# Whole-page gathers, input rows in three token tiles whose space the split output weights take, and first attention units without pacing

## The chip, the cores and the metric

The kernel runs on one core of a Trainium2 chip. The metric is device time in microseconds, from the first to the last instruction of one launch with what lies around it. The engines are TensorE (PE; its weight loads are shown as PEld), VectorE (DVE), ScalarE (ACT), GpSimd (POOL) and SyncE (SP). Each runs its own list of instructions in order. DMAs are issued from SP, ACT or POOL and run on 16 DMA engines. SyncE computes nothing; most DMAs are issued from it.

## What is computed

One step of a hybrid decoder layer, for a prompt of 1024 tokens and for 8 sample sequences of one new token each, all in float32. The reference, cut to what matters here:

```python
hn = rms_norm(x, norm_g)                           # 1024 + 8 rows of 1024
u, v, z_a, q, kc, vc, ks, vs, kw, vw, g, z_b = split(hn @ w_in)
a_out = u * spatial_gate(layer_norm(v)) * silu(z_a)
# per head: three attentions, weighted by gates and added
#   compressed blocks of kc/vc, selected blocks of ks/vs, a window of 512 of kw/vw
mix = concat([a_out, o_b * silu(z_b)], -1)
y = rms_norm(x + mix @ w_out, final_g)
# sample rows: k and v of the past come from pages, cache[page_table], 2 pages of 128 tokens each
pages = lambda c: c[page_table].reshape(B, past, N_KV, HEAD_DIM)
```

Two key/value heads serve 8 query heads. `compress` multiplies overlapping blocks of 32 keys with a weight. With 16 blocks of 64 tokens and 16 selected, every causal block is selected. Outputs are y for both parts and the new cache rows.

## The kernel before

**Products.** A float32 product is made from halves: each operand is split into a rounded float32r part ("hi") and the rest ("lo"), and three products hi·hi, hi·lo, lo·hi are added in PSUM. ACT makes hi by a cast, DVE or POOL makes lo by a subtraction.

**Stages** (times of the profiled execution). 0 to 116 us: `xw` (input rows transposed, next to the first weights) is loaded for eight slices k of the model dimension; the rows, times the norm weight, become `xh` and `xl` (lines 211, 212), each a tile of 8 x 1032 columns (1024 prompt tokens and 8 sample tokens). Feature tiles (`pf`) multiply 128 weight columns with all tokens in three pieces of `CH` = 344 columns. Then come token-major projections, nine row tiles each (eight of the prompt, one of the samples): V of the gMLP (`ptv`, with gate products `pg`), K tiles (`pta`, followed by transposes `pkt`), V tiles (`ptb`). From about 255 us `compress` runs for keys and values (transposes `pct`, product `pc`), then `sample_attention` (`pA`, `pB`, `pT`, `po`). From 361 us the prompt's attention runs in 32 units of two heads: eight blocks qb of 128 queries, four units each. A unit has scores (`S`), exponentials on ACT, weights times gate on DVE or POOL, transposes (`pt`) and values (`o`). The scores of unit i+1 are made while the values of unit i run. A score row covers 128 (qb+1) selected keys, up to 5 x 128 window keys and 64 compressed ones.

**Fill.** The remaining feature tiles (`feature_tiles`, two more u, three z and four b) are traced as fill for compress, the samples and the first 16 units. Later the output projection (`output`, `project`, `pout`) is the fill of units 18 to 31. Fill is traced with the lowest priority; a scheduler, when the program is built, sets the fixed order of each engine. `paced()` keeps fill products of a unit behind the last value product of the unit before (line 1196), and `held_back` (line 1200) keeps output products behind the last value product of unit 17.

**Pages and output weights.** `early(t, behind)` (line 386) is called once per row tile of V, K and V again, t = 0 to 23, behind a cast on ACT. It issues from ACT: the store of the last finished lo half of an output weight piece (line 389), page gathers (`gather`, lines 381 and 383), and for t < 16 the load of a 128 x 512 piece of `w_out` (line 398), which ACT casts (401) and POOL subtracts (402). The gather of a compressed page writes 256 rows of 512 bytes to `cg`; the gather of a selected page takes the two halves of 128 rows (k and p) and writes 512-byte rows to `kg`, so that `compress` and `sample_attention` read 8 KB rows (lines 688, 770, 795). When all 16 early units are traced, `woh` and `wol` take the space of `xh` and `xl` (tags wh and wl): `w_out` is loaded a second time, cast again on ACT (line 1205), and the lo halves are read back (1207).

Of the kernel before, what the change touches and what calls it, by code (L numbers as in the profile page):

```python
# [17 lines left out]
KT = 8  # L18
CH = 344
# [20 lines left out]
def trunk(tc, io, outs):  # L40
# [7 lines left out]
    with ExitStack() as top:  # L48
# [26 lines left out]
        cg = dram.tile([2, P, 16, P], F32, name="cg")  # L75
        kg = dram.tile([2, P, 16, P], F32, name="kg")
        wol_d = dram.tile([2, P, KT, 512], F32, name="wol_d")
# [53 lines left out]
        RSv = [RS[:, j * CH:(j + 1) * CH] for j in range(3)]  # L131
# [18 lines left out]
        def f_tiles(n):  # L150

            return [(ps_b if n % 2 else ps_s)("pf")[:, 0:CH] for _ in range(3)]
# [6 lines left out]
        def f_mm(hi, lo, outs, k, thirds=(0, 1, 2)):  # L159
            for (w, x, n) in ((hi, xh, 0), (hi, xl, 1), (lo, xh, 2)):  # L160
                for out, j in zip(outs, thirds):
                    last = mm(out, w, x[:, k, j * CH:(j + 1) * CH],
                       start=(k == 0 and n == 0), stop=(k == KT - 1 and n == 2))
            return last

        def views(t2d):
            return [t2d[:, j * CH:(j + 1) * CH] for j in range(3)]
# [30 lines left out]
        for k in range(KT):  # L198
# [5 lines left out]
            cuts = (0, wx + CH, wx + 2 * CH, wx + TT) if k == 0 else (0, wx + TT)  # L204
# [19 lines left out]
        first = [f_tiles(0), f_tiles(1), [ps_o("pf")[:, 0:CH], ps_p("pf")[:, 0:CH]]]  # L224
# [33 lines left out]
        rest = ps_s("pf")[:, 0:CH]  # L258
# [11 lines left out]
        g.tensor_copy(xsS[:, :, 0:8], f32(xh[:, :, T:TT]))  # L270
        xs_copy = g.tensor_copy(xsS[:, :, 32:40], f32(xl[:, :, T:TT]))
# [21 lines left out]
        for a, b in ((0, 2 * CH), (2 * CH, TT)):  # L293
            v.scalar_tensor_tensor(uz[:, 1, a:b], uz[:, 1, a:b] if a == 0 else rest, 0.5, RS[:, a:b],
                                   op0=ALU.mult, op1=ALU.mult)
# [83 lines left out]
        def gather(n):  # L379
            if n < 16:  # L380
                s.dma_start(cg[:, :, n, :], io["cA"][bass.ds(prow[n], 1)].rearrange("o k p c -> (o k) p c"))
            else:
                s.dma_start(kg[:, :, n - 16, :],
                            io["cB"][bass.ds(prow[n - 16], 1)].rearrange("o p (k c) -> (o k) p c", k=2))

        def early(t, behind):
            with tc.issue_after(behind.ins):
                if wo_low:
                    s.dma_start(*wo_low.pop())
                if t < 8:  # L390
# [4 lines left out]
                if t < 16:  # L395
                    half, k = t % 2, t // 2
                    st = wo.tile([P, 512], F32, tag="wost", name="wost")
                    s.dma_start(st, io["w_out"][k, :, half * 512:half * 512 + 512])
                    hi = wo.tile([P, 512], F32R, tag="wohi", bufs=1, name="wohi")
                    lo = wo.tile([P, 512], F32R, tag="wolo", name="wolo")  # L400
                    s.copy(hi, st)
                    g.tensor_tensor(lo, st, f32(hi), op=ALU.subtract)
                    wo_low.append((wol_d[half, :, k, :], f32(lo)))
# [7 lines left out]
        def t_tile(ps, wts, i, cols):  # L411
            if i < 8:
                sl = slice(i * P, (i + 1) * P)
                for k in range(KT):
                    hi, lo = wts[k]
                    mm(ps[:, :cols], xh[:, k, sl], hi[:, :cols], k == 0, False)
                    mm(ps[:, :cols], xh[:, k, sl], lo[:, :cols], False, False)
                    mm(ps[:, :cols], xl[:, k, sl], hi[:, :cols], False, k == KT - 1)
# [188 lines left out]
        def feature_tiles(bank):  # L607
# [5 lines left out]
            for n, (what, i, _) in enumerate(todo):  # L613
                wts = f_ahead.pop(0)
                if 0 < n < len(todo) - 1:
# [3 lines left out]
                for j in range(3):  # L619
                    ps = bank()("pf")[:, 0:CH]  # L620
                    for k in range(KT):
                        hi, lo = wts[k // 4]
                        c = (k % 4) * P
                        with tc.high_priority(FILL), paced():
                            at_bank[1] = f_mm(hi[:, c:c + P], lo[:, c:c + P], [ps], k, (j,))
                        if k % 2:
                            yield
                    if what == "u":
                        v.scalar_tensor_tensor(views(u)[j], ps, 0.5, RSv[j], op0=ALU.mult, op1=ALU.mult)
                        continue  # L630
                    n_p = CH if j < 2 else T - 2 * CH
                    cols = slice(j * CH, j * CH + n_p)
                    if what == "z":
                        gt = ftp.tile([P, CH], F32, tag="gt", bufs=2, name="gt")
                        sy.dma_start(gt[:, 0:n_p], sd[i, :, cols])
# [703 lines left out]
```

## Time and profile before

| | us |
|---|---|
| three runs | 743.98, 746.26, 746.06; median 746.06 |
| the profiled execution | 744.38 |
| its span, first to last instruction | 742.6 |
| PE busy | 693.6 |
| DVE busy | 509.1 |
| ACT busy | 383.0 |
| POOL busy | 293.1 |
| granted TensorE clock, mean | 0.967 |

The span holds 12,587 instructions and 91.29 MB of DMA traffic. PE's ends are modelled, so a busy PE may still be waiting a little. A granted clock of 1.00 is the upper level, 2.4 GHz; 0.50 is 1.2 GHz; a value between is a mean over the stretch.

### The profile page before, as it was taken

Reading aid. Unit: us, or ns where it says so; the run is one execution under the profiler, and the core shown is the slowest. Engines: PE = TensorE matmul, PEld = TensorE weight load, DVE = VectorE, ACT = ScalarE, POOL = GpSimd, SP = SyncE. Lnnn points to the kernel's source line nnn. Section 1 sums busy time; section 2 is a strip of 40 time slices with the busy share of each in tenths; the row PEclk is TensorE's granted clock in tenths of the full one; section 3 lists DMA queues with packets and bytes.
Section 4 is the critical chain, followed back from the end, with each engine's and each line's share of the span. In section 5 each row is a group of like instructions: output and inputs, shape, how many; then the busy total and the mean of one; then the engine's idle time right before and its main releaser. Section 6 shows DMA issues by size and latency. Waiting matters only on the chain.

```text
span 742.6 us, 12587 instructions
## 1 busy us (share of the span) xinstructions
PE 693.6 (93%) x4186; PEld 636.6 (86%) x4186; DVE 509.1 (69%) x1470; ACT 383.0 (52%) x906; POOL 293.1 (39%) x282
## 2 busy tenths in 40 slices
PE   9999998999779769999899999988999999999994
PEld 7999986889669769879799999967888988899893
DVE  5848883698362257542699878887868787878743
ACT  7614312232353454311577867797656675767631
POOL 0034224456122213333222544444756565556511
PEclk9999998999999979999799999998999999999997
DMA  9334655333654464172532112299133021122011
GB/s 330 105 141 171 164 125 159 118 107 122 215 162 147 133 190 161 48 294 72 145 90 78 62 49 63 78 387 263 44 101 99 31 85 60 44 72 72 15 57 56
DMA packets 69096, 91.29 MB, mean 123 GB/s; under 512 B 5872, under 2 KB 45408, under 8 KB 68232
## 3 DMA queue, kind: packets, MB, share of 16 engines
q1 hardware_dynamic: 55496, 75.48, 32.3%
q10 hardware_dynamic: 13376, 12.85, 5.5%
q0 software_dynamic: 160, 2.15, 0.8%
q8 instruction: 33, 0.54, 0.3%
q14 instruction: 31, 0.25, 0.1%
HBM read 67.85 MB, written 28.91 MB: 130 GB/s over the span
## 4 chain that ended last, share of the span: by engine, by line
PE 67%; DVE 9%; DMA 9%; issue 6%; ACT 4%; ACTq 2%; POOL 1%; SPq 0%; POOLq 0%; DVEq 0%
PE pf L45 15%; PE pout L45 12%; PE o L45 10%; PE S L45 9%; PE pt L978 8%; PE ptv L45 3%; PE pta L45 3%; DMA wst<-in_wF 2%; PE pg L45 2%; PE pc L45 2%; DVE wlo L144 2%; DMA wost<-in_w_out 1%; DMA wst<-in_w_c 1%; PE po L45 1%; DMA kg<-in_cB 1%
## 5 line engine op out<-in xcount | busy, mean ns | idle before, releaser
L982 DVE TENSOR_TENSOR tl<-pt,th 128x512 fp32r<-128x512 f32 (+1 forms) x160 | 101.1, 644 | 19.1 <-ACT th L981 18.2
L45 PE MATMUL pf<-xh,whi 128*128 128x344 f32 x384 | 109.0, 328 | 1.5 <-DVE mS L848 0.8
L45 PE MATMUL pf<-xl,whi 128*128 128x344 f32 x384 | 110.2, 325 | 0.0
L45 PE MATMUL pf<-xh,wlo 128*128 128x344 f32 x384 | 109.3, 324 | 0.0
L981 ACT CAST th<-pt 128x512 fp32r<-128x512 f32 (+1 forms) x160 | 85.0, 552 | 36.4 <-PE pt L978 30.7
L955 POOL TENSOR_TENSOR Pw<-Pw,r 128x640 f32<-128x640 f32 (+3 forms) x112 | 76.4, 701 | 49.6 <-DVE r L949 21.9
L45 PE MATMUL pout<-woh,mix 128*128 128x512 f32 (+1 forms) x272 | 88.3, 391 | 2.2 <-ACT mix L1015 1.8
L955 POOL TENSOR_TENSOR Pl<-Pl,r 128x384 f32<-128x384 f32 (+5 forms) x36 | 49.1, 1364 | 87.3 <-DVE r L949 56.0
L45 PE MATMUL o<-th,v 128*128 128x256 f32 x264 | 75.9, 307 | 2.6 <-DVE oT L991 2.2
L45 PEld LDWEIGHTS pf<-xh,whi 128*128 128x128 f32 x384 | 70.4, 192 | 3.0 <-ACT xh L211 1.6
L45 PEld LDWEIGHTS pf<-xl,whi 128*128 128x128 f32 x384 | 70.7, 191 | 1.3 <-issue 1.0
L45 PEld LDWEIGHTS pf<-xh,wlo 128*128 128x128 f32 x384 | 70.5, 191 | 0.4 <-issue 0.2
L45 PE MATMUL o<-tl,v 128*128 128x256 f32 x264 | 70.4, 292 | 0.4 <-DVE tl L982 0.3
L901 ACT ACTIVATE Pl<-Pl,nmx 128x128 f32<-128x128 f32 (+7 forms) x64 | 49.8, 779 | 26.8 <-DVE nmx L897 26.7
L45 PEld LDWEIGHTS pout<-woh,mix 128*128 128x128 f32 x272 | 51.0, 193 | 11.1 <-ACT mix L1015 2.0
L45 PE MATMUL S<-ksS,q 128*128 128x384 f32 (+5 forms) x192 | 54.3, 370 | 4.7 <-DVE nmx L897 2.2
L45 PE MATMUL S<-kwS,q 128*128 128x384 f32 (+2 forms) x224 | 55.6, 345 | 1.4 <-DVE nmx L897 1.0
L45 PEld LDWEIGHTS o<-th,v 128*128 128x128 f32 x264 | 51.2, 194 | 5.2 <-DVE oT L991 2.7
L941 ACT ACTIVATE Pw<-Pw,nmx 128x640 f32<-128x640 f32 (+4 forms) x64 | 44.6, 697 | 18.8 <-DVE nmx L933 17.9
L45 PEld LDWEIGHTS o<-tl,v 128*128 128x128 f32 x264 | 51.3, 194 | 3.2 <-DVE tl L982 1.9
L45 PE MATMUL pout<-wol,mix 128*128 128x512 f32 (+1 forms) x136 | 52.4, 386 | 0.0
L978 PE MATMUL pt<-ident,Pw 128*128 128x128 f32 x304 | 50.0, 276 | 0.4
(338 smaller groups left out, 1670.5 us busy)
## 6 DMA issues: line engine op xcount, KB each, us to landing
q<-qd SPq DMA_DIRECT2D x32, 256.0 KB
wst<-in_wF SPq DMA_DIRECT2D x26, 256.0 KB
raw<-in_xw SPq DMA_DIRECT2D x7, 708.0 KB
wost<-in_w_out ACTq DMA_DIRECT2D x16, 256.0 KB
wol_d<-wolo ACTq DMA_DIRECT2D x16, 256.0 KB
wol<-wol_d SPq DMA_DIRECT2D x2, 2048.0 KB
wost<-in_w_out SPq DMA_DIRECT2D x16, 256.0 KB
xt<-in_x_prompt SPq DMA_DIRECT2D x8, 512.0 KB
```

Source lines behind the costliest of these rows:

```text
L45: return pe.matmul(out, lhsT, rhs, start=start, stop=stop, skip_group_check=True)
L144: e.tensor_tensor(lo[:, :n], st[:, :n], f32(hi[:, :n]), op=ALU.subtract)
L901: s.activation(Pl[:, 0:L], Pl[:, 0:L], AF.Exp, bias=nmx[:, 0:1], scale=-1.0, accum_out=sums[:, 1:2])
L941: s.activation(Pw[:, 0:nw], Pw[:, 0:nw], AF.Exp, bias=nmx[:, 1:2], scale=-1.0, accum_out=sums[:, 2:3])
L955: g.tensor_tensor(t_[:, a:b], t_[:, a:b], r[:, j:j + 1].to_broadcast((P, b - a)), op=ALU.mult)
L978: pe.transpose(pt[:, ci * 256 + e * P:ci * 256 + (e + 1) * P], src[e][:, col:col + P], ident)
L981: s.copy(th[:, :n], pt[:, :n])
L982: v.tensor_tensor(tl[:, :n], pt[:, :n], f32(th[:, :n]), op=ALU.subtract)
```

## The change

Four edits, and what follows from them:

1. A page is gathered as it lies in the cache: 16 rows of 8 KB to `cg[j]` or `kg[j]`. The three readers sort: they read 512-byte pieces in a rearranged view. `early` gathers one compressed page per call for t < 16 and two selected pages per call for t = 16 to 23 (before: two compressed pages for t < 8 and one selected page for t = 8 to 23).
2. `early` keeps both halves of a `w_out` piece in one tile and stores both to `wod`. The second load of `w_out`, its 16 casts and the pool for them are gone.
3. The input rows lie in three tiles `X[0..2]` of 384, 384 and 264 tokens, hi and lo together. Feature tiles come in pieces of these widths. The last two feature tiles run alternately piece by piece; after each pair one token tile is free, and a DMA loads 6, 6 or 4 split weight pieces from `wod` into its space (`Wo`). `wo_part` finds a piece.
4. Fill of the first eight units is not paced. Output products start one unit earlier by the code: only unit 16 gets no fill, and they are held behind the last value product of unit 16.

```diff
-CH = 344
+CUT = (0, 384, 768, 1032)
+CW = (384, 384, 264)
...
-        xh = xp.tile([P, KT, TT], F32R, tag="wh", name="xh")
-        xl = xp.tile([P, KT, TT], F32R, tag="wl", name="xl")
+        X = [xp.tile([P, 2, KT, w], F32R, tag=f"x{j}", name=f"x{j}") for j, w in enumerate(CW)]
...
-                s.activation(xh[:, k, a:b], xs[:, a:b], AF.Copy, scale=ng[:, k:k + 1])
-                v.scalar_tensor_tensor(xl[:, k, a:b], xs[:, a:b], ng[:, k:k + 1], f32(xh[:, k, a:b]),
-                                       op0=ALU.mult, op1=ALU.subtract)
+                for j in range(3):
+                    if a <= CUT[j] < b:
+                        xj = xs[:, CUT[j]:CUT[j + 1]]
+                        s.activation(X[j][:, 0, k, :], xj, AF.Copy, scale=ng[:, k:k + 1])
+                        v.scalar_tensor_tensor(X[j][:, 1, k, :], xj, ng[:, k:k + 1], f32(X[j][:, 0, k, :]),
+                                               op0=ALU.mult, op1=ALU.subtract)
...
-        def gather(n):
-            if n < 16:
-                s.dma_start(cg[:, :, n, :], io["cA"][bass.ds(prow[n], 1)].rearrange("o k p c -> (o k) p c"))
-            else:
-                s.dma_start(kg[:, :, n - 16, :],
-                            io["cB"][bass.ds(prow[n - 16], 1)].rearrange("o p (k c) -> (o k) p c", k=2))
+        def gather(to, page, j):
+            s.dma_start(to[j], page[bass.ds(prow[j], 1)])
+
+        cA_rows = io["cA"].rearrange("n k (x p) c -> n (k x) (p c)", x=8)
+        cB_rows = io["cB"].rearrange("n (x p) c -> n x (p c)", x=16)
...
-                if t < 8:
-                    gather(2 * t)
-                    gather(2 * t + 1)
+                if t < 16:
+                    gather(cg, cA_rows, t)
+                    st = wo.tile([P, 512], F32, tag="wost", name="wost")
+                    s.dma_start(st, io["w_out"][t % 8, :, t // 8 * 512:t // 8 * 512 + 512])
+                    sp = wo.tile([P, 2, 512], F32R, tag="wosp", name="wosp")
+                    s.copy(sp[:, 0], st)
+                    g.tensor_tensor(sp[:, 1], st, f32(sp[:, 0]), op=ALU.subtract)
+                    wo_low.append((wod[:, t], f32(sp)))
                 else:
-                    gather(8 + t)
...
+                    gather(kg, cB_rows, 2 * t - 32)
+                    gather(kg, cB_rows, 2 * t - 31)
...
+            f_ahead.append(f_weights(todo[-1][2], g))
+            for j in range(3):
+                for (what, i, _), wts in zip(todo[-2:], f_ahead):
+                    yield from third(what, i, wts, u, j)
+                a, b = ((0, 6), (6, 12), (12, 16))[j]
+                Wo.append(xp.tile([P, b - a, 2, 512], F32R, tag=f"x{j}", name=f"wo{j}"))
+                sy.dma_start(f32(Wo[j]), wod[:, a:b])
...
+        def wo_part(k, hl, a, b):
+
+            n = a // 512 * 8 + k
+            return Wo[n // 6][:, n % 6, hl, a % 512:a % 512 + b - a]
...
-            sy.dma_start(cA, cg[kv])
+            sy.dma_start(cA, cg.rearrange("j (k x) (p c) -> k (x p) j c", k=2, c=P)[kv])
...
+        kg_rows = kg.rearrange("j x (p c) -> (x p) j c", c=256)
...
-            sy.dma_start(cK, kg[0])
+            sy.dma_start(cK, kg_rows[:, :, 0:P])
...
-            sy.dma_start(cV, kg[1])
+            sy.dma_start(cV, kg_rows[:, :, P:256])
...
-            if i:
+            if i >= 8:
                 pace[:] = [blocks[todo[i - 1][0]]["last"].ins]
             units = [n_values(q) + 2 for q, _, _ in todo[i:] if (q < EARLY) == (qb < EARLY)]
-            if 0 <= i - 4 * EARLY < 2:
+            if i == 4 * EARLY:
                 units[0] = 0
-            if i == 4 * EARLY + 2:
+            if i == 4 * EARLY + 1:
                 held_back = blocks[qb]["last"].ins
...
-                woh = xp.tile([P, KT, D], F32R, tag="wh", name="woh")
-                wol = xp.tile([P, KT, D], F32R, tag="wl", name="wol")
-                wo_ctx = ExitStack()
-                wop = wo_ctx.enter_context(tc.tile_pool(name="wop", bufs=10, side="right", reuse_waits="tile"))
-                for half in range(2):
-                    cs_ = slice(half * 512, half * 512 + 512)
-                    for k in range(KT):
-                        st = wop.tile([P, 512], F32, tag="wost", name="wost")
-                        sy.dma_start(st, io["w_out"][k, :, cs_])
-                        s.copy(woh[:, k, cs_], st)
-                        if k == (7 if half == 0 else 1):
-                            sy.dma_start(f32(wol[:, :, cs_]), wol_d[half])
-                wo_ctx.close()
```

What stands in a row on three engines' lists, before and now. First ACT, where the first K tiles leave PSUM (`ka`, `kvc`), are split for the transposes (`k`), and `early` stands between. Before:

```order
L535 ACTIVATE ka<-pta,rs 128x256
L536 ACTIVATE kvc<-pta,rs 128x128
L546 CAST k_2006<-ka 128x4x64
L389 DMA wol_d<-wolo 128x512
L383 ISA
L383 DMA kg<-in_cB 256x1x128
L398 DMA wost<-in_w_out 128x512
L546 CAST k_2059<-ka 128x4x64
...
L401 CAST wohi<-wost 128x512
```

Now, at the same tiles:

```order
L535 ACTIVATE ka<-pta,rs 128x256
L536 ACTIVATE kvc<-pta,rs 128x128
L546 CAST k_2019<-ka 128x4x64
L391 DMA wod<-wosp 128x1024
L383 ISA
L383 DMA cg<-in_cA 16x2048
L395 DMA wost<-in_w_out 128x512
L546 CAST k_2071<-ka 128x4x64
...
L552 CAST ksS<-pkt 128x2x128
...
L397 CAST wosp<-wost 128x512
```

The same steps stand in the same order; the selected page in 256 rows is now a compressed page in 16, the store is twice as wide, and the cast of the staged weights comes later.

Second PE, where the first unit's scores begin (`q_3685` and `q_3859` before, `q_3698` and `q_3872` now, are the queries of its two key/value heads). Before:

```order
L45 MATMUL pf<-xh,wlo 128x344
L45 MATMUL S<-ksS,q_3685 128x128 x2
L45 MATMUL S<-kwS,q_3685 128x192 x2
...
L45 MATMUL S<-ksS,q_3859 128x128 x2
L45 MATMUL S<-kwS,q_3859 128x192 x2
...
L978 MATMUL pt<-ident,Pl 128x128
L978 MATMUL pt<-ident,Pw 128x128
```

Now:

```order
L46 MATMUL S<-ksS,q_3698 128x128 x2
L46 MATMUL S<-kwS,q_3698 128x192 x2
...
L46 MATMUL pf<-x_107,whi 128x384 x2
L46 MATMUL pf<-x_107,wlo 128x384
...
L998 MATMUL pt<-ident,Pl 128x128
L998 MATMUL pt<-ident,Pw 128x128
...
L46 MATMUL S<-ksS,q_3872 128x128 x2
L46 MATMUL pf<-x_108,whi 128x264 x2
L46 MATMUL pf<-x_108,wlo 128x264
```

Between the scores now stand feature products, 69 of them up to the end of unit 0's values, where none stood. In units 4 to 7 none stand now, where there were 70.

Third PE, at the first output product (`q_6231` before: queries of block 5, first head; `q_5866` now: block 4, second head). Before:

```order
L978 MATMUL pt<-ident,Pw 128x128 x6
L45 MATMUL S<-kwS,q_6231 128x384 x2
L45 MATMUL S<-ksS,q_6231 128x384 x2
L45 MATMUL pout<-woh,mix 128x512
L45 MATMUL pout<-wol,mix 128x512
```

Now:

```order
L46 MATMUL S<-kwS,q_5866 128x384 x2
L46 MATMUL S<-ksS,q_5866 128x320 x2
L46 MATMUL o<-tl,vc_1932 128x256
L998 MATMUL pt<-ident,Pl 128x128 x2
L998 MATMUL pt<-ident,Pw 128x128 x2
L46 MATMUL pout<-wo_4977,mix 128x512 x12
```

From the last feature product to the first output product there were 84 value products (`o`); now there are 40, two units less.

## Rows read from the trace of the kernel before

**Rows 1.** The page's first part: busy us, share of the span, instructions.

```profile
PE 693.6 (93%) x4186; PEld 636.6 (86%) x4186; DVE 509.1 (69%) x1470; ACT 383.0 (52%) x906; POOL 293.1 (39%) x282
```

**Rows 2.** Busy time of each engine by stretch: stretch, its length, then PE, PEld, DVE, ACT, POOL with instruction counts, the granted clock, the DMA share, GB/s.

```profile
116.00:180.00 64.00, 59.49 (x313) 52.72 (x312) 45.48 (x129) 16.80 (x29) 35.84 (x31) 0.95 0.39 119
180.00:260.00 80.00, 65.67 (x359) 62.24 (x358) 32.23 (x95) 31.53 (x81) 18.76 (x16) 0.95 0.53 163
260.00:361.20 101.20, 91.12 (x555) 84.88 (x553) 50.51 (x93) 32.49 (x64) 32.24 (x31) 0.95 0.48 158
361.20:387.80 26.60, 26.27 (x157) 24.85 (x155) 24.25 (x140) 21.07 (x87) 4.83 (x13) 0.81 0.28 79
387.80:414.00 26.20, 26.10 (x192) 25.50 (x191) 24.32 (x97) 20.69 (x68) 8.81 (x16) 1.00 0.29 83
414.00:481.80 67.80, 67.65 (x496) 66.28 (x496) 57.57 (x206) 49.83 (x138) 31.26 (x42) 1.00 0.21 60
481.80:494.60 12.80, 12.00 (x79) 9.87 (x78) 12.70 (x52) 10.73 (x27) 6.17 (x8) 1.00 1.05 390
494.60:521.60 27.00, 22.25 (x125) 18.15 (x123) 19.79 (x68) 22.84 (x59) 12.00 (x13) 0.87 0.93 276
533.30:708.40 175.10, 174.39 (x1070) 156.20 (x1069) 135.25 (x412) 113.36 (x244) 101.07 (x85) 1.00 0.22 69
```

**Rows 3.** PE's waits over the whole span: what waited, for whom, us in total, times, the longest.

```profile
PE pkt L551 <- DVE k L548: 7.0, 3, 4.6
PE pc L45 <- ACT Xh L697: 5.7, 1, 5.7
PE pct L703 <- DVE kccs L594: 4.5, 1, 4.5
PE pta L45 <- ACT kvc L536: 2.6, 1, 2.6
```

**Rows 4.** ACT's timeline among the K and V tiles: start, duration, then what; ACTq is the issue of a DMA on ACT's queue; in brackets the idle time before and what ended it.

```profile
187.45 2.48 ACTq L398 DMA_DIRECT2D wost<-in_w_out  x1
190.04 0.40 ACT L546 CAST k<-ka 128x256 fp32r<-128x256 f32 x1 [4.00 <-DMA wol_d<-wolo]
190.88 5.16 ACTq L398 DMA_DIRECT2D wost<-in_w_out  x1
196.09 0.62 ACT L401 CAST wohi<-wost 128x512 fp32r<-128x512 f32 x1 [5.64 <-DMA wost<-in_w_out]
...
235.03 3.28 ACTq L383 DMA_DIRECT2D kg<-in_cB  x1
```

**Rows 5.** The chain that ended last, in order of time, between 180 and 281 us: start, us, what.

```profile
190.88 9.44 DMA wost<-in_w_out
...
252.27 5.06 DMA out<-vb
...
259.59 7.95 DMA wst<-in_w_c
```

**Rows 6.** ACT's timeline at the first V tiles, and a store's issue.

```profile
121.71 0.61 ACTq L398 DMA_DIRECT2D wost<-in_w_out  x1
...
122.51 1.19 ACTq L381 DMA_DIRECT2D cg<-in_cA  x2
...
124.87 0.62 ACT L401 CAST wohi<-wost 128x512 fp32r<-128x512 f32 x1 [1.89 <-DMA cg<-in_cA]
...
136.29 0.33 ACTq L389 DMA_DIRECT2D wol_d<-wolo  x1
```

**Rows 7.** As rows 2, a stretch of 3 us among the V tiles.

```profile
238.00:241.00 3.00, 3.00 (x18) 3.00 (x17) 0.00 (x0) 0.62 (x1) 1.29 (x1) 1.00 0.14 43
```

**Rows 8.** Line 1205: duration ns least, median and most, first and last start in us.

```profile
L1205 ACT CAST woh<-wost x16: 603/628/651, 489.4 to 514.2; 128x512 fp32r<-128x512 f32 x16
```

**Rows 9.** The chain that ended last: runs of products without a wait between, start, us, what, how many.

```profile
10.56 30.52 PE pf L45 x192
...
165.76 9.63 PE pta L45 x55
...
414.24 1.32 PE pt L978 x12
...
562.81 1.43 PE o L45 x12
...
692.38 1.17 PE S L45 x6
```

**Rows 10.** As rows 2, of the instructions of one tile alone: S, then o, then pt.

```profile
494.60:521.60 27.00, 9.95 (x36) 5.76 (x34) 8.91 (x21) 0.87 0.93 276
494.60:521.60 27.00, 9.58 (x45) 7.64 (x45) 0.81 (x2) 0.74 (x2) 0.87 0.93 276
494.60:521.60 27.00, 7.27 (x44) 5.58 (x44) 7.97 (x13) 6.29 (x12) 0.87 0.93 276
```

**Rows 11.** DVE's groups of instructions from 387.8 to 414.0 us, those of the features: line, shapes, count, busy us, mean ns.

```profile
L640 DVE SCALAR_TENSOR_TENSOR z<-th,z 128x344 f32<-128x344 f32 x3 | 2.2, 722 | 0.0
L638 DVE TENSOR_TENSOR z<-pf,RS 128x344 f32<-128x344 f32 x3 | 1.5, 502 | 0.0
```

More of the change, by code (lines that the diff above doesn't have):

```diff
@@ L150, in f_tiles @@
         def f_tiles(n):
-            return [(ps_b if n % 2 else ps_s)("pf")[:, 0:CH] for _ in range(3)]
+            return [(ps_b if n % 2 else ps_s)("pf")[:, 0:w] for w in CW]
         def f_k(wts, outs3, k):
@@ L159, in f_mm @@
         def f_mm(hi, lo, outs, k, thirds=(0, 1, 2)):
-            for (w, x, n) in ((hi, xh, 0), (hi, xl, 1), (lo, xh, 2)):
+            for (w, x, n) in ((hi, 0, 0), (hi, 1, 1), (lo, 0, 2)):
                 for out, j in zip(outs, thirds):
-                    last = mm(out, w, x[:, k, j * CH:(j + 1) * CH],
+                    last = mm(out, w, X[j][:, x, k, :],
                        start=(k == 0 and n == 0), stop=(k == KT - 1 and n == 2))
@@ L166, in views @@
         def views(t2d):
-            return [t2d[:, j * CH:(j + 1) * CH] for j in range(3)]
+            return [t2d[:, a:b] for a, b in zip(CUT, CUT[1:])]
         wa_ctx = ExitStack()
@@ L612, in feature_tiles, with third @@
             sy.dma_start(u, ud)
-            for n, (what, i, _) in enumerate(todo):
+            def third(what, i, wts, u, j):
+                ps = bank()("pf")[:, 0:CW[j]]
+                for k in range(KT):
+                    hi, lo = wts[k // 4]
+                    c = (k % 4) * P
+                    with tc.high_priority(FILL), paced():
+                        at_bank[1] = f_mm(hi[:, c:c + P], lo[:, c:c + P], [ps], k, (j,))
+                    if k % 2:
+                        yield
+                if what == "u":
+                    v.scalar_tensor_tensor(views(u)[j], ps, 0.5, RSv[j], op0=ALU.mult, op1=ALU.mult)
+                    return
+                w, n_p = CW[j], min(CW[j], T - CUT[j])
+                cols = slice(CUT[j], CUT[j] + n_p)
+                if what == "z":
+                    gt = ftp.tile([P, CW[0]], F32, tag="gt", bufs=2, name="gt")
+                    sy.dma_start(gt[:, 0:n_p], sd[i, :, cols])
+                z = ftp.tile([P, CW[0]], F32, tag="z", bufs=3, name="z")[:, 0:w]
+                th = ftp.tile([P, CW[0]], F32, tag="th", name="th")[:, 0:w]
+                v.tensor_tensor(z, ps, RSv[j], op=ALU.mult)
+                s.activation(th, z, AF.Tanh, scale=0.5)
+                v.scalar_tensor_tensor(z, th, 1.0, z, op0=ALU.add, op1=ALU.mult)
+                if what == "z":
+                    g.tensor_tensor(z, z, views(u)[j], op=ALU.mult)
+                    if j == 2:
+                        v.tensor_tensor(as_[:, i, :], z[:, n_p:w], ss_[:, i, :], op=ALU.mult)
+                    g.tensor_tensor(z[:, 0:n_p], z[:, 0:n_p], gt[:, 0:n_p], op=ALU.mult)
+                elif j == 2:
+                    v.tensor_copy(zs[:, i, :], z[:, n_p:w])
+                sy.dma_start((ad if what == "z" else zd)[i, :, cols], z[:, 0:n_p])
+            for n, (what, i, _) in enumerate(todo[:-2]):
                 wts = f_ahead.pop(0)
-                if 0 < n < len(todo) - 1:
+                if n:
                     f_ahead.append(f_weights(todo[n + 1][2], g))
@@ L631, in feature_tiles @@
[L631 to L635, printed above, removed]
-                    z = ftp.tile([P, CH], F32, tag="z", bufs=3, name="z")
-                    th = ftp.tile([P, CH], F32, tag="th", name="th")
-                    v.tensor_tensor(z, ps, RSv[j], op=ALU.mult)
```

77 lines of the change are left out of this document (25 added, 52 removed).

## The prediction

> **What bounds the kernel now.** Read the page's busy shares first: TensorE (PE) is busy 93% of the span, VectorE (DVE) 69% [rows 1]. So an edit pays only where PE stands still or runs at the lower of its two clock levels. The table of stretches then shows where that is [rows 2]. From 414 to 481.8 us and from 533.3 to 708.4 PE is busy for all but 0.9 us at a granted clock of 1.00: nothing is to be had. Three stretches are worse: 180 to 260 (PE busy 65.7 of 80.0 us, clock 0.95), 260 to 361 (91.1 of 101.2, clock 0.95), and 494.6 to 521.6 (22.3 of 27.0, clock 0.87). Third, PE's own list of waits names who ends them [rows 3]: transposes of the K tiles (pkt, 7.0 us), the compress product (pc, 5.7), its transposes (pct, 4.5), the K projection waiting for its PSUM bank (pta, 2.6). All stand between 185 and 277 us. Behind each the reader finds ScalarE (ACT).
>
> ACT is busy 31.5 of 80 us there [rows 2]: not full but held. Its timeline shows DMA issues of 2.48 and 5.16 us, with computing instructions late behind them [rows 4]. The chain of waits shows transfers of a strange length: 9.44 us for a 256 KB load, 5.06 for a 64 KB store, 7.95 for a 256 KB weight load [rows 5]. Earlier, from 120 to 128 us, such a load is issued at 121.71 and used at 124.87, so 3.2 us [rows 6]. Meanwhile the DMA engines are not full. From 238 to 241 us their share is 0.14, which is 2.2 of 16 engines, and 43 GB/s [rows 7]. The last DMA that ACT issued before it is a kg gather [rows 4]. I read this so: a gather of a selected page runs on about two engines (43/2.2 = 19 GB/s each, so 128 KB takes 3 us or more); 16 of them in 75 us keep those two occupied, and every transfer has a share on them, so all end late.
>
> The Trainium skill (DMA: Bandwidth & Descriptors, "Why a DMA increments its semaphore by 16 and not by 1") says that a DMA is split over the largest number of engines, at most 16, that divides the slowest dimension of both its sides. The old gather walks 2 halves of 128 rows, so two engines: the trace's 2.2 agrees.
>
> **The change, part by part.**
>
> *Page gathers.* A page now goes as 16 rows of 8 KB, issued by ACT, instead of 256 pieces of 512 bytes. ACT's issue time: two old gathers cost 1.19 us, a 128-row store 0.33 [rows 6]; at 0.3 the 32 gathers save 32 x 0.3 = 9.6 us of ACT, off the path except where ACT is late. The larger term is the crowd on two engines. If the 16 rows spread, each gather lasts about 128 KB/(16 x 19) = 0.4 us and the crowd is gone. Then, by the rows:
> (a) pkt and pta, 9.6 us [rows 3]: they follow ACT's held issues. ACT also waits there for its own staging loads of the output weights, which stay, so I take two thirds, 6.5.
> (b) pct, 4.5: behind the 64 KB store of 5.06 us; at most 3.2 for it gives at least 1.9, and its issue comes earlier too; 3.5.
> (c) pc, 5.7: behind the 7.95 us weight load; 7.95 - 3.2 = 4.7; I take 4.5.
> (d) clock: 0.05 x 80 + 0.05 x 101 = 9 us are lost to the lower level [rows 2], after the stalls; I take 5.5.
> Sum 20 us. Low end 8 (a third of a, half of b and c, 1 of d), high end 26 (nearly all).
> Moved with it: selected pages two per V tile behind all compressed ones; last use is far later (cK is loaded after 315), cost nothing. Sorting on load: four 1 MB loads in 512-byte pieces. At 19 GB/s and 16 engines that is 3.4 us each; the best neighbouring stretch moved 390 GB/s [rows 2], 2.7 us. The 0.7 each hides under feature matmuls; kept as 0 to 3.
>
> *Write-back of both halves.* 16 stores of 512 KB instead of 256 KB, on ACT's queue: 4 MB more over 140 us. The share in 180 to 260 is 0.53 [rows 2]; there is room. 0, up to 3.
>
> *Output weights taken one by one.* Gone from 478 to 515 us: 16 loads of 256 KB, two of 2 MB, and 16 casts of 0.63 us on ACT [rows 8], 10 us of it, beside a DMA share of 1.05 [rows 2]. The first output product, which stood among the scores of block 5's first half, now stands among those of block 4's second: two units of four per block earlier. These two units, 494.6 to 521.6, had no fill. Price their PE work: 45 x 0.119 (o) + 36 x 0.195 (S) + 44 x 0.110 (pt) = 5.4 + 7.0 + 4.8 = 17.2 us [rows 9, 10], so 9.8 of 27.0 are standstill or lower clock. Output products fill that, and later units are shorter by as much, since they are PE-bound. With 1 us for the lighter ACT in the unit before and 1 off for the start, I take 10. Ends: 5 (the mix inputs come late) and 13 (the unit before gains too). The three new loads queue on SP while features still run; x0 and x1 are free one tile's third before the end. The q loads behind them are issued at least a unit ahead: 0.
>
> *Three tiles by tokens.* 384 + 384 + 264 columns instead of 3 x 344. A 344-wide product takes 30.52/192 = 0.159 us, a 384-wide 9.63/55 = 0.175, a 256-wide 0.119 [rows 9]: 0.175 x 2 + 0.122 = 0.472 against 0.477. Nothing. At the start ACT and DVE get 14 more instructions each; per k ACT then needs about 3.3 us while PE needs 24 x 0.159 = 3.8, so PE hides it: 0, at most 1.5.
>
> *First blocks unpaced.* By the order, unit 0 now holds 69 feature products (none before), and units 4 to 7 hold none (70 before). DVE is the limit here: 24.3 of 26.6 and 24.3 of 26.2 us [rows 2]. Features cost DVE little: 3 x (0.50 + 0.72) = 3.7 us in units 4 to 7 [rows 11], so attention alone keeps it 20.5 us, 5.1 per unit. New time: unit 0 69 x 0.159 + 4 = 15; units 1 to 3 as before, 16; units 4 to 7 between 5.1 and 6.5 each, 20 to 26. Sum 51 to 57 against 52.8: the filled hole at the start comes back as an unfilled one. I take +2, ends -3 and +6.
>
> **Sum.** 744.4 (this execution, span 742.6) - 20 - 10 + 2 = 716.4. The median of the runs, 746.1, lies 1.7 above it, so **718**.
>
> **The rivals.**
> 1. *ACT stays late.* ACT runs in order and still waits for staging loads, for GpSimd's subtraction before each store, and now has twice the bytes to store. For it: at 190 us ACT waits 4.0 us for such a store [rows 4]. Against: from 116 to 180 us the same steps run with PE busy 59.5 of 64.0 [rows 2]. Then the first term is its low end, 8: 746.1 - 8 - 10 + 2 = 730.
> 2. *The projection starts no earlier in fact*: the last feature stores stand behind the 2 MB weight load on SP, mix comes late, and PE waits in order with scores behind it. For it: 2 MB at 390 GB/s is 5.4 us. Against: a whole unit of about 12 us lies between. Second term 3: 725.
> 3. *A page goes over one engine* (slower). If 16 long rows were not spread, 128 KB at 19 GB/s takes 6.7 us, 32 pages 215 us on one engine, within the 140 us from 120 to 260 in which they are issued. Past 140/32 = 4.4 us a page, that engine is the bound; everything with a share on it is 75 us late: about 746 - 10 + 75 = 811. For it: the two-engine gather shows that spreading is not given. Against: no gather of the trace runs on one. By the rule of the Trainium skill cited above, 16 rows go over 16 engines, which is against it as well.
> 4. *Gains eaten*: first term 8, second 5, unpacing +6, the small costs 7: 746, no change.
>
> **How the numbers follow.** My forecast 0.72 (708 to 728 by its own), rival 1 0.13, rival 2 0.06, rival 3 0.05, rival 4 0.04. The range reaches from nearly all best ends (746 - 26 - 13 - 3 = 704) past rivals 1 and 2 to 738 (746 - 8 - 5 + 5). A difference over 0.3% (2.2 us) is what a measurement can tell: faster 0.72 + 0.13 + 0.06 = 0.91, same 0.04, slower 0.05.
>
> **What would show it.** Right: no ACT issue above 1.5 us from 185 to 260; weight loads of 3 to 4 us; PE's waits for pkt, pct and pc together under 8 us; the first pout some 25 us sooner after the last feature product; no clock below 1.00 around 510. Units 4 to 7 with PE idle and DVE full show the price of unpacing; if they are shorter than 22 us, I was wrong there. If the DMA share stays near 0.1 while ACT waits, the pages are not spread. A first output product that waits for mix speaks for rival 2.

## The result, and the profile after

The changed kernel took 710.25 us (median of four runs, 708.44 to 710.72) against 745.8 for the kernel before (four runs; the three shown ahead have a median of 746.06): ratio 0.952 (95% interval 0.950 to 0.955), 35.6 us less. The forecast was 718 with a range of 704 to 738. The profiled execution took 708.44 us, its span is 706.7.

The first part of the page after answers to [rows 1]:

```profile
PE 674.1 (95%) x4186; PEld 623.3 (88%) x4186; DVE 514.1 (73%) x1484; ACT 376.4 (53%) x904; POOL 297.7 (42%) x282
```

Where the time went is best read from landmarks, the starts of single products in the trace, since they hold whatever the order in between. "S" is the first score product, "u7" the last value product of unit 7, and so on; times in us. The rows below "after" are experiments, told further down.

| run | first pta | first pct | S | u7 | u15 | u18 | u31 | span |
|---|---|---|---|---|---|---|---|---|
| before | 149.9 | 251.7 | 360.9 | 414.0 | 481.8 | 521.6 | 727.5 | 742.6 |
| after | 148.0 | 238.7 | 339.1 | 392.1 | 459.7 | 497.3 | 692.6 | 706.7 |
| rows first | 150.3 | 240.1 | 338.0 | 391.3 | 459.2 | 497.8 | 703.7 | 718.0 |
| whole pages | 150.0 | 239.5 | 339.2 | 392.2 | 460.1 | 499.1 | 705.0 | 721.4 |
| contiguous halves | 149.1 | 240.6 | 337.4 | 391.8 | 459.4 | 497.3 | 692.6 | 708.2 |
| two engines | 150.8 | 252.6 | 381.6 | 435.8 | 503.4 | 540.4 | 735.6 | 750.3 |
| no casts | 148.0 | 240.2 | 336.7 | 389.8 | 457.8 | 489.1 | 694.9 | 709.8 |
| output later | 150.5 | 243.0 | 343.7 | 397.9 | 465.5 | 501.0 | 699.7 | 713.8 |
| casts back | 149.2 | 241.4 | 342.1 | 396.3 | 463.9 | 502.0 | 695.0 | 709.3 |
| paced | 149.0 | 240.3 | 338.9 | 389.6 | 456.7 | 490.6 | 692.5 | 707.2 |

From before to after: 1.9 us less up to the first K product, 19.9 less from there to the scores (211.0 to 191.1), 0.1 less in units 0 to 7, 0.2 less in units 8 to 15, 12.8 less from u15 to u31 (245.7 to 232.9), 1.0 less behind: 35.9 in all. So the two large terms of the forecast are the two large gains, and the rest is nothing.

The stretches after, with the columns of [rows 2]; the lines stand for the V and first K tiles, the K and V tiles, compress with the samples, units 0, 1 to 3 and 4 to 7, 8 to 15, and 16, 17 and 18:

```profile
116.00:180.00 64.00, 56.73 (x306) 50.94 (x307) 52.48 (x131) 18.42 (x34) 37.49 (x33) 0.97 0.40 132
180.00:238.70 58.70, 57.70 (x334) 56.05 (x333) 30.13 (x86) 27.98 (x73) 17.29 (x13) 1.00 0.83 272
238.70:339.10 100.40, 94.52 (x582) 88.14 (x581) 49.51 (x97) 34.56 (x68) 35.71 (x31) 0.98 0.53 163
339.10:355.10 16.00, 15.97 (x115) 15.96 (x115) 13.09 (x78) 10.70 (x47) 4.12 (x7) 1.00 0.33 100
355.10:370.10 15.00, 15.00 (x112) 14.97 (x111) 14.21 (x69) 11.71 (x45) 2.77 (x6) 1.00 0.27 83
370.10:392.10 22.00, 18.59 (x123) 15.40 (x122) 21.84 (x93) 18.73 (x64) 7.04 (x14) 1.00 0.29 82
392.10:459.70 67.60, 67.56 (x494) 65.54 (x492) 60.04 (x207) 49.36 (x138) 31.60 (x45) 1.00 0.44 155
459.70:472.00 12.30, 10.83 (x73) 9.24 (x72) 12.16 (x44) 9.86 (x27) 8.10 (x10) 1.00 1.01 327
472.00:484.00 12.00, 11.97 (x74) 10.85 (x75) 8.38 (x32) 7.88 (x20) 9.82 (x10) 1.00 0.27 93
484.00:497.30 13.30, 13.30 (x87) 12.22 (x86) 9.93 (x32) 8.45 (x20) 8.06 (x9) 1.00 0.37 103
```

The second line is the change in one row. It ends at the first `pct`; up to the same product the kernel before shows:

```profile
180.00:251.70 71.70, 61.84 (x336) 58.69 (x334) 30.11 (x86) 28.62 (x73) 18.76 (x16) 0.95 0.54 169
```

For as many products PE is now busy 57.7 of 58.7 us at a clock of 1.00, where it was 61.8 of 71.7 at 0.95, and the DMA share is 0.83 where it was 0.54. From the first K product to the first `pct` that is 11.1 of the 19.9 us (101.8 to 90.7). PE's waits after, with the columns of [rows 3]:

```profile
PE pg L46 <- ACT vh L482: 3.5, 1, 3.5
PE pc L46 <- ACT Xh L715: 2.8, 1, 2.8
PE pg L46 <- DVE sp L453: 2.1, 1, 2.1
...
PE pg L46 <- DVE vl L483: 1.3, 2, 0.9
...
PE pct L721 <- DVE kc__2984 L743: 0.5, 1, 0.5
...
PE pta L46 <- DVE wlo L144: 0.3, 1, 0.3
```

The K transposes (`pkt`, 7.0 us before) are gone from the list; `pc` and `pct` are left with 3.3 us together. New are 3.4 us of `pg` behind DVE, at 171 to 179 us. ACT's timeline at the K tiles after shows the same steps as [rows 4]:

```profile
186.20 0.51 ACTq L383 DMA_DIRECT2D cg<-in_cA  x1
186.75 0.75 ACTq L395 DMA_DIRECT2D wost<-in_w_out  x1
...
191.30 0.62 ACT L397 CAST wosp<-wost 128x512 fp32r<-128x512 f32 x1 [0.69 <-DMA wost<-in_w_out]
```

An issue that took 2.5 and 5.2 us takes 0.75, and ACT's wait for the staged weights at this place is 0.69 us instead of 5.64.

### The profile page after: what moved, and what is told of

It reads as the page before. It is cut to its first block, busy times and chain, and to the rows that moved or that the text cites. A ratio compares the mean times of both kernels' runs of the same rounds, so it can differ in the third digit from the quotient of the medians.

```text
span 706.7 us, 12576 instructions
## 1 busy us (share of the span) xinstructions
PE 674.1 (95%) x4186; PEld 623.3 (88%) x4186; DVE 514.1 (73%) x1484; ACT 376.4 (53%) x904; POOL 297.7 (42%) x282
## 4 chain that ended last, share of the span: by engine, by line
PE 59%; DVE 20%; DMA 7%; issue 5%; ACT 3%; POOL 3%; SPq 2%; ACTq 1%; POOLq 0%; DVEq 0%
PE pf L46 16%; PE pout L46 12%; PE o L46 8%; PE pt L998 7%; PE S L46 7%; PE ptb L46 5%; DVE tl L1002 2%; DVE Pl L917 2%; DVE Pw L953 1%; DVE wlo L144 1%; PE po L46 1%; DVE sp L453 1%; PE pA L46 1%; DVE raw L327 1%; DMA q<-qd 1%
## 5 line engine op out<-in xcount | busy, mean ns | idle before, releaser
L46 PE MATMUL pf<-x,whi 128*128 128x384 f32 (+1 forms) x768 | 173.6, 325 | 0.9 <-DVE mS L868 0.8
L46 PEld LDWEIGHTS pf<-x,whi 128*128 128x128 f32 x768 | 130.4, 190 | 2.9 <-PE poT L865 0.9
L46 PE MATMUL pf<-x,wlo 128*128 128x384 f32 (+1 forms) x384 | 111.6, 322 | 0.0
L46 PE MATMUL pout<-wo,mix 128*128 128x512 f32 (+1 forms) x408 | 101.2, 384 | 1.8 <-ACT mix L1035 1.8
L46 PEld LDWEIGHTS pout<-wo,mix 128*128 128x128 f32 x408 | 71.8, 188 | 14.1 <-ACT mix L1035 2.0
L46 PEld LDWEIGHTS pf<-x,wlo 128*128 128x128 f32 x384 | 69.9, 189 | 0.7 <-issue 0.6
L46 PE MATMUL S<-kwS,q 128*128 128x384 f32 (+2 forms) x224 | 52.7, 333 | 0.6 <-DVE nmx L917 0.4
L998 PE MATMUL pt<-ident,Pl 128*128 128x128 f32 x288 | 47.0, 273 | 1.0 <-DVE Pl L973 0.6
L143 ACT CAST whi<-wst 128x512 fp32r<-128x512 f32 (+2 forms) x50 | 28.0, 585 | 26.3 <-DMA wst<-in_wTa 8.2
L144 POOL TENSOR_TENSOR wlo<-wst,whi 128x512 fp32r<-128x512 f32 x18 | 23.9, 1331 | 40.9 <-ACT whi L143 39.0
```

The costliest lines, as they stand in the source:

```text
L46: return pe.matmul(out, lhsT, rhs, start=start, stop=stop, skip_group_check=True)
L143: s.copy(hi[:, :n], st[:, :n])
L144: e.tensor_tensor(lo[:, :n], st[:, :n], f32(hi[:, :n]), op=ALU.subtract)
L998: pe.transpose(pt[:, ci * 256 + e * P:ci * 256 + (e + 1) * P], src[e][:, col:col + P], ident)
```

## The experiments

All times are medians; each group of runs on one chip had its own runs of the kernel before (medians 743.35, 743.89 and 742.98 us), and ratios are to those.

**Rows first.** The kernel before, with one thing changed: which dimension of a page's transfer is outermost.

```diff
-                s.dma_start(cg[:, :, n, :], io["cA"][bass.ds(prow[n], 1)].rearrange("o k p c -> (o k) p c"))
+                s.dma_start(cg[:, :, n, :].rearrange("k p c -> p k c"),
+                            io["cA"][bass.ds(prow[n], 1)].rearrange("o k p c -> p (o k) c"))
...
-                s.dma_start(kg[:, :, n - 16, :],
-                            io["cB"][bass.ds(prow[n - 16], 1)].rearrange("o p (k c) -> (o k) p c", k=2))
+                s.dma_start(kg[:, :, n - 16, :].rearrange("k p c -> p k c"),
+                            io["cB"][bass.ds(prow[n - 16], 1)].rearrange("o p (k c) -> (o p) k c", k=2))
```

> The kernel before; a page still goes as 256 pieces of 512 bytes, in the same calls, but the 128 rows are the outermost dimension on both sides instead of the 2 halves. Every engine's order stays as it was. Theory (a transfer whose outermost dimension is 2 runs on two DMA engines and crowds them): most of the first term comes back here, 746 - 16 to 21 = 725 to 730, no ACT issue above 1.5 us from 185 to 260. Rival (it is the 512-byte pieces, 256 for a page, that make a gather slow): 744 to 748, with the long ACT issues as before.

Measured: 718.94 us, ratio 0.967 (0.963 to 0.972). Same bytes, same 256 pieces of 512 bytes, same calls, and 22.9 us are gone at the first score (360.9 to 338.0), as much as in the changed kernel (339.1). The time lies 6 us below the range that was expected. No ACT issue between 100 and 300 us is above 1.3 us. The rival that blames small pieces falls. The same transfers, by DMA issue (tile, count, KB each, median us from issue to landing):

```profile
cg<-in_cA ACTq DMA_DIRECT2D x16, 128.0 KB, 2.8
kg<-in_cB ACTq DMA_DIRECT2D x16, 128.0 KB, 2.6
```

Which pages ran otherwise before? The trace files keep every semaphore update that a DMA made; these are counts over the files and stand in no view. For the same 343 transfers there are 5196 updates before and 5404 here, 208 fewer before. Taken semaphore by semaphore, the difference is 13 for each of the 16 selected pages (`kg`) and none for a compressed page (`cg`). So the edit changed the running of the selected pages alone, and before it only those 16 ran on few engines. That fewer updates stand for fewer engines is read from this and from the share of 2.2 engines in [rows 7]; no trace names the engines. Why the compressed pages were spread already is not shown; their two halves follow each other in memory on both sides, as in the run with contiguous halves below.

**Whole pages.** The kernel before with edit 1's form alone, at the old places:

```diff
-                s.dma_start(cg[:, :, n, :], io["cA"][bass.ds(prow[n], 1)].rearrange("o k p c -> (o k) p c"))
+                s.dma_start(cg[n], cA_rows[bass.ds(prow[n], 1)])
...
+                s.dma_start(kg[n - 16], cB_rows[bass.ds(prow[n - 16], 1)])
...
-            sy.dma_start(cA, cg[kv])
+            sy.dma_start(cA, cg.rearrange("j (k x) (p c) -> k (x p) j c", k=2, c=P)[kv])
...
```

> The kernel before with whole-page gathers (16 rows of 8 KB) and sorted loads alone, at the old places: two compressed pages per call for t < 8, one selected page for t = 8 to 23. Theory: as the run with rows outermost, 724 to 730. Rival (part of the gain after comes from where the pages stand now, or from the start, the stores or the unpaced units): 732 to 742. If the sorted loads cost something, this run is slower than the one with rows outermost by that much, 0 to 3 us.

Measured: 722.92 us, 0.971 (0.966 to 0.975), just below the range of the theory. The first score comes at 339.2: the whole first term again. That pages stand elsewhere after the change, and in pairs, gave nothing that shows. The time is 4 us above the run with rows first, and the intervals overlap.

**Contiguous halves.** The changed kernel with a page as 2 x 8 rows:

```diff
-            s.dma_start(to[j], page[bass.ds(prow[j], 1)])
+            s.dma_start(to[j].rearrange("(h r) c -> h r c", h=2),
+                        page[bass.ds(prow[j], 1)].rearrange("o (h r) c -> (o h) r c", h=2))
```

> The changed kernel; each page goes as 2 halves of 8 rows of 8 KB, so that the outermost dimension is 2 and all else, the orders of all engines too, stays. Theory (two DMA engines): 710 + 14 to 22 = 724 to 732, long ACT issues and late weight loads are back. Rival (number and size of the pieces): 709 to 712.

Measured: 709.93 us, 0.955 (0.951 to 0.959). By the order of the built kernel the instruction still reads 16 x 2048: halves that follow each other were merged into one row dimension, and the trace has as many semaphore updates by DMAs as the changed kernel, 5164. So it tells nothing of engines; it is a second measurement of the changed kernel, 709.93 beside 710.25.

**Two engines.** The same with halves that can't be merged:

```diff
-            s.dma_start(to[j].rearrange("(h r) c -> h r c", h=2),
-                        page[bass.ds(prow[j], 1)].rearrange("o (h r) c -> (o h) r c", h=2))
+            s.dma_start(to[j].rearrange("(r h) c -> h r c", h=2),
+                        page[bass.ds(prow[j], 1)].rearrange("o (r h) c -> (o h) r c", h=2))
```

> The changed kernel; a page goes as two interleaved halves (rows 0, 2, 4 ... and rows 1, 3, 5 ..., 8 rows of 8 KB each), so that its outermost dimension is 2 and can't be merged with the rows. In the run with two contiguous halves it was merged when built, to the same 16 rows as in the changed kernel, so that run was a repeat. All orders stay. Theory (a transfer runs on as many engines as its outermost dimension divides into, here two): 710 + 14 to 24 = 724 to 734, with long ACT issues among the K and V tiles. Rival (with 8 KB rows two engines are enough, the crowd was one of many small pieces on two engines): 709 to 714.

Measured: 750.66 us, 1.008 (1.005 to 1.011). With 16 rows of 8 KB and an outermost dimension of 2 the changed kernel is 40 us slower, 0.8% above the kernel before. Nearly all of it lies between the K tiles and the scores (S 42.5 us later than after; S to u31 354.0 against 353.5). PE's waits in this run, then its chain:

```profile
PE pct L722 <- DVE kccs L595: 18.1, 1, 18.1
PE pc L46 <- ACT Xh L716: 12.5, 1, 12.5
```

```profile
225.16 14.14 DMA out<-vb
...
244.37 11.59 DMA kg<-in_cB
...
256.03 8.06 DMA wod<-wosp
...
264.11 8.55 DMA out<-vb
```

A page of 128 KB takes 11.6 us, a 64 KB store 14.1, and the transposes wait for them through ACT. In one stretch of 3 us of this hole, with the columns of [rows 2], PE does nothing and the DMA engines run at a share of 0.20 (3.2 of 16); over the whole hole, 252.6 to 297.3 us, the share is 0.43:

```profile
270.00:273.00 3.00, 0.00 (x0) 0.00 (x0) 0.00 (x0) 0.18 (x1) 0.00 (x0) 0.50 0.20 73
```

The expectation missed twice. The size, 14 to 24 us, was taken from the crowd of the kernel before, and this one is larger: 4748 semaphore updates by DMAs against 5164 in the changed kernel are 13 fewer for each of 32 pages, where 16 were affected before, and the selected pages are issued within 51 us (225.1 to 276.3) instead of 72 (186.2 to 258.1). And no ACT issue is long here (all under 1.4 us). The held issues of [rows 4] came with many small pieces on two engines; the late transfers need only the two engines.

**Small pieces.** The changed kernel with gathers of 512-byte pieces, rows first, into the old sorted layout, and no sorting on load:

```diff
-            s.dma_start(to[j], page[bass.ds(prow[j], 1)])
+            s.dma_start(to[:, :, j, :].rearrange("k p c -> p k c"), page[bass.ds(prow[j], 1)].rearrange("o p k c -> (o p) k c"))
...
-            sy.dma_start(cA, cg.rearrange("j (k x) (p c) -> k (x p) j c", k=2, c=P)[kv])
+            sy.dma_start(cA, cg[kv])
...
```

> The changed kernel with gathers of 512-byte pieces, rows outermost, into the sorted layout of before, and loads that read 8 KB rows: nothing is sorted on load. If the sorted loads cost what the prediction allows (0 to 3 us) and small pieces nothing: 707 to 711. If the pieces cost ACT or the queues something: 711 to 715.

Measured: 709.63 us (705.63 to 714.51), 0.954 (0.950 to 0.958): as the changed kernel. Copying pages whole and sorting them later is worth nothing by itself; what is worth some 20 us is the outermost dimension, and either form has it.

**Unsorted.** The price of the sorted loads:

```diff
-            sy.dma_start(cA, cg.rearrange("j (k x) (p c) -> k (x p) j c", k=2, c=P)[kv])
+            sy.dma_start(cA.rearrange("p j c -> p (j c)"), cg.rearrange("j y w -> (j y) w")[kv * P:kv * P + P])
```

> The changed kernel; the two 1 MB loads of the compressed pages read 8 KB rows as they lie, so the past keys come unsorted into compress and the sample rows are computed from wrong keys. What the sorting on load costs: by the prediction 0 to 1.5 us for the two, 708 to 710; if the 6.7 us of a sorted load stands before the compress product, 704 to 708.

Measured: 707.76 us, 0.951 (0.948 to 0.954), not to be told from the changed kernel: 0 to 3, as forecast.

**No casts.** The kernel before with rows first, and edit 2: both halves of the output weights stored early and loaded whole, still into two tiles that come free only when the features end.

```diff
...
-                    for k in range(KT):
-                        st = wop.tile([P, 512], F32, tag="wost", name="wost")
-                        sy.dma_start(st, io["w_out"][k, :, cs_])
-                        s.copy(woh[:, k, cs_], st)
-                        if k == (7 if half == 0 else 1):
-                            sy.dma_start(f32(wol[:, :, cs_]), wol_d[half])
+                    sy.dma_start(f32(woh[:, :, cs_]), wol_d[half, :, :, 0])
+                    sy.dma_start(f32(wol[:, :, cs_]), wol_d[half, :, :, 1])
...
```

> The kernel before with gathers that have the 128 rows outermost, and with both halves of the output weights stored in early and loaded whole (four loads of 1 MB on SP): the 16 loads of 256 KB and the 16 casts on ACT are gone from 478 to 515 us. Input rows stay in two tiles, output products start with unit 19 as before. New theory for the second term (ACT with 10 us of casts and the loads ahead of them made units 16 to 18 slow, not the missing fill): 719 - 6 to 10 = 709 to 713. Rival (the earlier start, as the prediction has it): 716 to 720.

Measured: 712.32 us, 0.959 (0.955 to 0.963), 6.6 below the run with rows first (the four loads are of 2 MB each, not 1 MB). Output products still start with unit 19 (the first at 490.1 us, behind the last value product of unit 18 at 489.1), and yet units 16 to 18 fall from 38.6 to 31.3 us; from u18 to u31 both runs need 205.8 or 205.9. Units 16, 17 and 18 in this run, then in the kernel before, with the columns of [rows 2]:

```profile
457.80:469.20 11.40, 10.62 (x73) 8.88 (x71) 11.30 (x42) 7.92 (x21) 6.09 (x7) 1.00 1.04 387
469.20:477.90 8.70, 7.81 (x57) 6.86 (x55) 8.54 (x32) 6.57 (x18) 4.06 (x5) 1.00 1.05 388
477.90:489.10 11.20, 9.41 (x61) 8.63 (x59) 8.97 (x29) 7.94 (x20) 7.21 (x9) 0.85 1.10 305
```

```profile
481.80:494.60 12.80, 12.00 (x79) 9.87 (x78) 12.70 (x52) 10.73 (x27) 6.17 (x8) 1.00 1.05 390
494.60:506.50 11.90, 9.76 (x61) 7.34 (x60) 8.95 (x34) 10.13 (x27) 5.39 (x6) 1.00 1.05 337
506.50:521.60 15.10, 12.49 (x66) 10.82 (x64) 10.84 (x37) 12.71 (x33) 6.61 (x7) 0.77 0.83 228
```

The DMA share is no lower (1.04 to 1.10, against 0.83 to 1.05); ACT's busy time is 11.1 us less over the three units. So a good part of what I took for missing fill went with the casts and the small loads, without any fill.

**Output later.** The changed kernel with the output's start moved back one unit:

```diff
-            if i == 4 * EARLY:
+            if 0 <= i - 4 * EARLY < 2:
...
-            if i == 4 * EARLY + 1:
+            if i == 4 * EARLY + 2:
```

> The changed kernel, with output products starting one unit later: units 16 and 17 get none, and they are held behind the last value product of unit 17. The loads and casts of the output weights stay gone. Theory (most of the second term is fill for the units that had none): 710 + 5 to 9 = 715 to 719. Rival (the 16 casts, 16 loads and two long loads that are gone made these units slow): 709 to 712.

Measured: 714.13 us, 0.960 (0.956 to 0.964); the changed kernel in the shape with contiguous halves had 709.93 beside it. This is below the 715 to 719 of the theory. And of the 4 us only about 1.2 lie where the edit acts (u15 to u31 234.2 against 232.9 and 233.1). The first score is late by 4.6 and 6.3 us against these two traces, though no instruction before unit 16 differs. One unit of fill is worth little.

**Casts back.** The changed kernel, the 16 casts put back on ACT in units 16 to 18:

```diff
...
+                for n in range(16):
+                    s.copy(sink, fg[:, n // 8 * 512:n // 8 * 512 + 512])
```

> The changed kernel with 16 casts of 128x512 put back on ACT, at the start of unit 16 by the code, from a resident tile (no loads, and nobody reads the result); output products start with unit 17 as in the changed kernel. If ACT's 10 us of casts alone made units 16 to 18 slow: 710 + 4 to 8 = 714 to 718. If it was the wait of the casts for their loads, or the later start of the output alone: 709 to 712.

Measured: 711.58 us, 0.956 (0.953 to 0.960), within the error of the changed kernel. By the landmarks u15 to u31 takes 231.0 us (232.9 after). Only two of the casts stand in unit 16, which has no fill; 14 stand in units 17 and 18. Units 17 and 18 of this run:

```profile
476.40:490.00 13.60, 13.60 (x87) 12.43 (x87) 11.01 (x39) 13.55 (x35) 10.61 (x11) 1.00 0.36 114
490.00:502.00 12.00, 12.00 (x78) 10.94 (x77) 9.60 (x26) 11.28 (x24) 6.90 (x8) 1.00 0.26 75
```

In unit 17 ACT is busy 13.55 of 13.60 us, and PE has no hole: with fill, the casts cost nothing that shows. So the casts alone do not make a unit slow; casts in units without fill do, or their loads. No run separates these two. The traces show one wait of ACT for such a load in these units, 1.7 us before and 1.4 us with rows first, so the loads' part that can be seen is small.

**Paced, and paced from unit 4.** The changed kernel with one line changed, as below in the first run, and to `if i >= 4:` in the second:

```diff
-            if i >= 8:
+            if i:
```

> The changed kernel with the fill of all units but the first paced again (no feature products in unit 0, 70 in units 4 to 7). By the prediction unpacing costs 2 us, so this run is at 706 to 709. By the two traces' first eight units (52.8 us before, 49.5 after, both from the start of the first scores) unpacing gives about as much as the feature products that it brings forward cost: 709 to 713.

> The changed kernel with fill unpaced in units 0 to 3 alone: 48 feature products in unit 0, none in units 1 to 3, 72 in units 4 to 7. If the 3.4 us that TensorE is idle in units 4 to 7 of the changed kernel can be filled without opening a hole in units 1 to 3: 705 to 708. If the hole only moves: 709 to 712.

Measured: 711.49 us (0.956; 0.951 to 0.960) and 711.61 (0.956; 0.952 to 0.960). Neither differs from the changed kernel by more than the intervals: taking the unpacing back gains nothing in the whole time. (The 49.5 us of the first expectation count from 342.6 us; from the first score at 339.1 they are 53.0.) In the trace of the paced run units 0 to 7 take 50.7 us instead of 53.0, and u15 to u31 takes 235.8 instead of 232.9: the output products stand otherwise there, and the gain is given back. Paced from unit 4, the hole moves to units 1 to 3: PE is busy 11.3 of 13.4 us there, and 27.2 of 27.2 in units 4 to 7. Unit 0 of the paced run and of the kernel before, both without fill:

```profile
338.90:347.10 8.20, 7.51 (x46) 5.92 (x47) 7.68 (x61) 7.42 (x39) 1.20 (x4) 1.00 0.52 140
```

```profile
360.90:371.30 10.40, 10.11 (x45) 9.03 (x46) 8.79 (x66) 8.01 (x40) 1.21 (x4) 0.55 0.35 93
```

The hole of unit 0 cost more before because TensorE's granted clock was at 0.55 there, near the lower level; in the paced run it stayed at 1.00.

**Low half.** The price of storing both halves:

```diff
...
-                    wo_low.append((wod[:, t], f32(sp)))
+                    wo_low.append((wod[:, t], f32(sp[:, 1])))
...
-                sy.dma_start(f32(Wo[j]), wod[:, a:b])
+                for hl in range(2):
+                    sy.dma_start(f32(Wo[j][:, :, hl]), wod[:, a:b])
```

> The changed kernel, in which only the lo halves of the output weights are stored (16 x 256 KB instead of 16 x 512 KB) and then loaded for both halves, so that the output product is made with lo in the place of hi. Price of the second half of the store: by the prediction 0 to 3 us, so 707 to 711. If the 4 MB more on ACT's queue hold the weight loads from 116 to 260 us: 702 to 707.

Measured: 712.83 us, 0.956 (0.952 to 0.960): 4 MB less to store gain nothing; the time is above both ranges that were expected. None of these versions is faster than the changed kernel by more than its interval.

## Why the prediction held, and where its sizes were off

**Page gathers: right, cause and size.** Forecast 20 us, measured 19.9 from the first K product to the first score. That they agree to 0.1 us is luck: with the same order of instructions this stretch took 188.4 to 193.2 us in four further traces (contiguous halves, output later, casts back, low half), so the gain is 18 to 23, against a single trace before. The parts, which add up to 21: (a) 9.6 us of waits for `pkt` and `pta` fell to 0.3, more than the 6.5 taken, but 3.4 us of `pg` behind DVE came in their place; (b) 4.0 for 3.5; (c) `pc`, 5.7 and 1.7 behind ACT and DVE before, has 3.1 left, so 4.3 for 4.5; (d) the clock lost 0.05 x 181 = 9 us before and 0.02 x 100 = 2 after, 7 for 5.5. That it is the spreading is shown from both sides: rows first alone, with the small pieces kept, brings it, and whole rows on two engines take away twice as much, with twice as many pages there. The Trainium skill (DMA: Bandwidth & Descriptors, "Why a DMA increments its semaphore by 16 and not by 1") has the number of engines from the outermost dimension of both sides, "as the instruction carries it"; both runs agree, and so does the run whose halves were merged. Rival 1 (ACT stays late, this term at 8 us) falls with the 19.9. Rival 3 (811 us for pages on one engine) was not tried; the run on two engines shows its mechanism, a crowd that makes the other transfers late.

**Output weights: right to within 3 us, the working mis-sized.** Forecast 10, measured 12.8. The step that failed is its split: 1 us for the lighter ACT and 9.8 for fill. (The row itself has 4.8 us without PE and 0.13 x 27.0 = 3.5 at the lower clock, 8.3; the 9.8 came from counted products.) The runs show 7.4 us without any earlier output (u15 to u31 244.5 to 237.1, rows first against no casts), and then 2.9 for a start with unit 18 and 1.3 more for unit 17 (237.1, 234.2, 232.9, though the first of these steps holds the other edits too). With fill, 16 casts cost nothing. So it was one hole: fill closes it with the casts in place, dropping the casts and the small loads closes 7.4 us of it without fill, and the two do not add. Whether casts or loads opened it stays open: the run that put the casts back has no loads. Rival 2 (the projection waits for mix) did not come: the one wait of `pout` for mix is 1.8 us at 694.7, as it was at 729.6 before.

**First blocks unpaced: the stage as forecast, the +2 not.** Units 0 to 7 took 53.0 us, in the forecast 51 to 57, and 22.0 of it in units 4 to 7 with DVE busy 21.84 and PE 18.59, as said. But the kernel before took 53.0 too, so against it the term is nothing. The prediction's list of bad stretches left out 361.2 to 387.8 us, which [rows 2] has at a clock of 0.81: with fill in unit 0 it is 1.00 there, and what that gives is what the hole in units 4 to 7 costs. The paced run had 1.00 in unit 0 without fill; why the clock stayed up there is not shown. Against that run unpacing costs 2.3 us in these units, but in the whole time it can't be told from nothing, since what pacing gains at the start is given back behind unit 15.

**What was kept at nothing.** Sorted loads, double store and small pieces: each run that takes one away, or puts it back, lies within the interval. The three token tiles have no run of their own; up to the first K product the kernels with the old tiles needed 148.0 to 150.3 us and those with the new 147.9 to 150.8, so the 1.9 us won there are the spread of executions.

The sum for the profiled execution was 716.4, the changed one took 708.4. The 8.0 us between are 2.8 of the output term, 2.3 in units 0 to 15 (the 2 forecast as a loss, and 0.3 gained), 1.9 of spread at the start and 1.0 at the end. The signs named ahead came as stated but for one: the median from issue to landing was 4.0 to 5.3 us for the weight loads, not 3 to 4, which came from one load at 121.71 us whose wait, by [rows 6], a page gather ended. PE's waits for `pkt`, `pct` and `pc` fell below 4 us, and the first output product came 17.4 us after the last feature product (45.5 before).

## What to carry to other kernels

Look at a transfer's outermost dimension before the size of its pieces: 128 or 16 spread, 2 did not, and one view written the other way round was worth 24 us here. Long transfers at a low DMA share are the sign, and the other transfers suffer with the culprit. When an engine stands still in a stretch, ask whether filling it and removing its cause are the same gain: here they did not add.

## What the runs showed of the hardware that I had not expected

Rows of 8 KB did not help the pages on two engines: one on the chain took 11.6 us, where one in pieces of 512 bytes took 7.9 before:

```profile
223.95 7.88 DMA kg<-in_cB
```

With 32 such pages for 16, issued closer together, the two do not compare piece with row. The time that ACT needs to issue a DMA stayed under 1.4 us in the run on two engines, so a normal issue time is no proof of a free queue. And the same instructions up to unit 15 reached the first score at 337.4 us in one execution and at 343.7 in another, which is why differences of 2 to 4 us between whole runs decide nothing here and landmarks within a stage do.
